# One-hot gate matrices stored token by token, 128 contiguous values a token, with indices and gates in pairs

## The chip, the cores and the metric

The kernel runs on one core of one Trainium2 chip. The metric is the device time of one launch in microseconds (us); lower is better. A core has five engines with instruction streams of their own: TensorE (PE in the views; PEld is its loading of stationary operands, "weights"), VectorE (DVE), ScalarE (ACT), GpSimd (POOL) and SyncE (SP), which here issues the transfers of the weight stream.

## The reference, cut to what matters

A first block (gated mixers and a feed-forward net) is followed by two layers, a retention layer and a latent attention layer, each with a product-key expert net behind it. The change lies in the expert net, which runs twice on 256 tokens. Each token has 8 heads with 16 chosen experts each, so 128 chosen experts of 16384; an expert's number is 128 * i1 + i2.

```
s1, i1 = lax.top_k(s[:, :, 0], PEER_TOPK)
s2, i2 = lax.top_k(s[:, :, 1], PEER_TOPK)
...
top_s, pos = lax.top_k(cand_s, PEER_TOPK)
eidx = jnp.take_along_axis(cand_i, pos, axis=-1)
gate = jax.nn.softmax(top_s, axis=-1).astype(xb.dtype)
h = jax.nn.gelu(jnp.einsum('thkd,td->thk', u[eidx], xb), approximate=False)
return jnp.einsum('thk,thkd->td', gate * h, v[eidx])
```

The kernel does not gather. It computes gelu(u x) for all 16384 experts, multiplies it by a dense gate that is zero for the experts that were not chosen, and multiplies by v.

## The kernel before

The whole net is one program, in an order written out by hand: each engine executes its instructions in the order in which the code emits them. Weights come as units of 128x1024 float32. For each unit SP issues a transfer to `raw` (L138, four units ahead), ScalarE rounds it to `whi` (L149), VectorE subtracts to get the rest `wlo` (L164), and TensorE does three products a tile to get float32 accuracy (L221, L222 and L223 for 256 moving columns, L285 to L287 for 512). Rounding and subtraction run up to two units ahead of the products; `whi` and `wlo` have three buffers each.

`peer` is the expert net of one layer. It has three parts: the query product with the choice of experts in the background (`topk`), a loop over 128 tiles `e` of the u product (24 products each, one unit of weight), and the v product, again 128 units.

`topk` leaves four tiles with a row for each of a token's 128 chosen experts and a column for each of the 256 tokens: `i1h` and `i2h` (the two halves of the expert's number), `gh` and `gl` (the gate as a float16 and the float16 rest). ScalarE writes `i1h`, `i2h` (L1215) and `gh` (L1232) from PSUM, VectorE writes `gl` (L1233).

The dense gate is made beside the u product, four tokens at a time, 64 groups a layer. A group has three steps:

- `g_onehot`, on VectorE, four instructions of 128x512 float16: `o1` is 1 where the first half of the index equals the column's number (L1252), `o2` the same for the second half (L1253), and `ohh` and `ohl` are `o2` times the two parts of the gate (L1254, L1255). `o1`, `ohh` and `ohl` have two buffers, `o2` one. All four have the shape [128, 128, 4]: the value for number i and token j of the four lies at position 4 i + j, so the 128 values of one token are 4 elements (8 bytes) apart.
- `g_mm`, on TensorE, eight products of 128x128 float16: for each of the four tokens `ohh` (L1265) and `ohl` (L1266) are loaded as the stationary operand and `o1` streams as the moving one, both read with that step of 4 elements. The eight go behind the 24 products of one tile `e`.
- `g_evac`, which brings the group's gates out of PSUM: VectorE multiplies them into the tiles of `X` that already hold gelu (L1276), ScalarE copies them to the places of the tiles still to come (L1278).

In tile `e` the code emits the 24 products of `e`, the eight products of the group whose one-hots were built beside the tile before, and then `finish(e - 1)`: gelu on ScalarE (L1294, L1296), the evacuation of the group multiplied beside tile `e - 1`, the one-hots of the next group, and the product of gelu and gate (L1302). Last come the rounding and the subtraction of the weight of tile `e + 2`. One-hots begin once the background work of `topk` is done (about tile 46), and a schedule spreads the 64 groups over the tiles up to 123, so some tiles have none.

A short loop `keep_warm` (L293) elsewhere in the program multiplies a constant float16 tile `idle`, 384 moving columns, with contiguous operands; nobody reads its result.

Of the kernel before, what the change touches and what calls it, by code (L numbers as in the profile page):

```python
# [10 lines left out]
F32 = mybir.dt.float32  # L11
# [19 lines left out]
# weight streams in the order in which they are used: (input, units, columns)  # L31
# [12 lines left out]
# per-feature vectors, one column for each 128 features  # L44
# [13 lines left out]
# constants that depend on the shapes alone  # L58
# [15 lines left out]
# units whose product is one float32 matmul a tile, where VectorE is the busier engine  # L74
# [18 lines left out]
def fused_kernel(ctx: ExitStack, tc: tile.TileContext, a: dict, out: bass.AP):  # L93
# [12 lines left out]
    # ---------------------------------------------------------------- constants  # L106
    cst = const.tile([P, NCST], F32, name="cst")
    vec = const.tile([P, NVEC], F32, name="vec")
    io = const.tile([P, 768], F16, name="io")
    iota4 = io[:, 0:512].rearrange("p (i t) -> p i t", t=4)  # L110
    iota16 = io[:, 512:768].rearrange("p (r k) -> p r k", r=16)
# [15 lines left out]
    # ---------------------------------------------------------------- weight stream  # L127
# [41 lines left out]
    def pump(budget):  # L169
        """emit background work worth the budget in us of VectorE; the work yields its cost, or None when it must wait."""  # L170
        if not bg:
            return
        st["credit"] = min(st["credit"] + budget, 2.0)
        i = 0
        while st["credit"] > 0 and i < len(bg):
            try:
                c = next(bg[i])
            except StopIteration:
                bg.pop(i)
                continue  # L180
            if c is None:
                i += 1
            else:
                st["credit"] -= c

    def drain_bg(*gens):
        """emit all that is left of these generators, or of all of them."""
# [10 lines left out]
    def take(name, i):  # L198
        """the next unit; nothing is split ahead for it."""
# [15 lines left out]
    # ---------------------------------------------------------------- products  # L215
# [3 lines left out]
    def mm3(ps, w, x, start, stop):  # L219
        """ps += w_tile^T x to float32 accuracy, w and x as (hi, lo)."""  # L220
# [4 lines left out]
    def steps(stages, n):  # L225
        """the stages of n items, the later stages of an item emitted beside the earlier ones of the next."""
# [6 lines left out]
    def lin_fm(name, xhl, nk, nf, evac, k0=0, budget=0.0, head=0, produce=None, post=None, i0=0, f_base=0, x32=None):  # L233
        """out^T[f] = sum_k W[k, f]^T x^T[k]; the weight comes as 8 tiles a unit, f major.
        The first `head` output tiles go k by k, as the k tiles of x are produced."""
# [46 lines left out]
    def tm_half(w, ps, o, xh, xl, ncol, first, last):  # L282
        """ps[128 tokens, cols o..o+512] += x[k]^T W[k] for one block of tokens."""
# [5 lines left out]
    def keep_warm(n):  # L289
        """products of a constant that nobody reads: the tensor engine's clock stays up while a norm is worked out."""  # L290
# [4 lines left out]
    def lin_tm(name, x_of, nk, ncol=1024, i0=0, budget=0.0, mid=None, after=None, psb=None, each=None, lead=0, warm=0):  # L295
        """token-major out = x W; x_of(k, b) gives the (hi, lo) stationaries of k tile k, token block b.
        Returns the banks [block][half of the columns]; `mid` comes before the last but one unit, `after` at the end."""
# [23 lines left out]
    # ---------------------------------------------------------------- small pieces  # L321
# [7 lines left out]
    def rstd_of(x, n):  # L329
        """1/sqrt(x) for a small [P, n] tile of positive numbers."""  # L330
# [12 lines left out]
    def table_ready(func=AF.Sqrt):  # L343
        """have the function's table in place."""
        nc.scalar.activation(out=small("rt", 1), in_=eps_t[:, 0:1], func=func)

    def rstd_root(v, scale, eps, ahead=False):
        """1/sqrt(scale * v + eps) for v [P, 2]; ScalarE may round a weight ahead behind the root."""
# [8 lines left out]
    def recip_root(s, x, n):  # L357
        """1/sqrt(x) from s = sqrt(x): the reciprocal and one Newton step."""
# [7 lines left out]
    def ln_coeffs(rows, eps, root=False, ahead=False):  # L366
        """rstd and -mean*rstd [P, 2] of the token-major rows of the two blocks, each in chunks of at most 512."""
# [12 lines left out]
    def coeffs_of(mv, eps, root=False, ahead=False):  # L380
        """the same from mv [P, block, (mean, variance)]."""
# [9 lines left out]
    def rms_coeff(rows, n, eps, junk):  # L391
        """rstd [P, 2] of the mean squares of the token-major rows of the two blocks."""
# [10 lines left out]
    def transposes(src, k, ps):  # L403
        """ps[128 features, 256 tokens] from the token-major src [P, 2, *], feature tile k."""
# [6 lines left out]
    def diags(r, pool):  # L411
        """diagonal matrices of the two columns of r."""
# [7 lines left out]
    def spread(dgs, dst):  # L420
        """dst[:, token] = the diagonals' values, on every partition."""
# [5 lines left out]
    def add_alpha_h(psb, h):  # L427
        """out[token, feature] += ALPHA * h."""
# [13 lines left out]
    class LnTail:  # L442
        """layer norm of token-major PSUM rows into the feature-major h and its split, block by block."""
# [23 lines left out]
    # ================================================================ sin and cos  # L467
    def sincos(ang, sn, cs, pool, n, c1=0.9, c2=1.2):
        """sn, cs of ang >= 0, step by step; ang is overwritten."""
# [18 lines left out]
    # ================================================================ first block  # L488
# [27 lines left out]
    def sq_mm(sq, k, ssp):  # L516
        """ssp[token, block] += sum over the features of tile k."""
# [4 lines left out]
    def rms_of(ssp, n, eps, root=False):  # L522
        """rstd [token, block] from the sums of squares."""
# [31 lines left out]
    # conv branch: a * sigmoid(gate), then the depthwise taps and the statistics in the background  # L555
# [34 lines left out]
    # the same token-major, in the place of the inputs  # L590
# [31 lines left out]
    # pooling branch: token-major here, so that the windows are products over the tokens  # L622
# [28 lines left out]
    def sgu():  # L651
        """mixed^T[c, i] = sum_j v[j, c] w_s[i, j] + b_s, times u; the norm's gain and bias of c are applied to the product."""
# [69 lines left out]
    # pooling branch  # L722
# [23 lines left out]
    # conv branch: layer norm over the channels, silu  # L746
# [16 lines left out]
    class RmsTail:  # L763
        """h_out = h_in + rms_norm(rows) * g, feature-major, from token-major PSUM rows."""
# [23 lines left out]
    # feed-forward; its norm's rstd is applied to the products  # L788
# [56 lines left out]
    # tables of the retention layer, in the background  # L845
    def tables():
# [11 lines left out]
        # log gamma = log1p(-exp(l)), then the decay between key m (partition) and query n  # L858
# [43 lines left out]
    # gated per-layer embedding  # L902
# [42 lines left out]
    # ================================================================ retention  # L945
# [32 lines left out]
    def ret_y(hd, pss):  # L978
        """rows of head hd, token-major"""
# [5 lines left out]
    def ret_n(hd, step):  # L985
        """their norm, in three steps"""
# [11 lines left out]
    def ret_t(f):  # L998
        """feature-major, gated and split: three steps, for feature tiles f, f-1 and f-2"""
# [16 lines left out]
    for hf in range(2):  # L1016
# [8 lines left out]
        if hf == 0:  # L1025
            # scores^T[m, n] * decay
# [26 lines left out]
    # ================================================================ product-key experts  # L1053
    NCAND = 80  # sums of the rank pairs (0, 0..15), (1..7, 0..7), (8..15, 0): they hold the 16 greatest of the 256
    NEG = -3.0e38

    def peer(layer, hl, lt, hm, scope, after_of, mid_of=None, beside_v=()):
        """experts of one layer; lt produces hl during the first product. after_of(X) gives the tail's callback."""
# [6 lines left out]
        def open_x():  # L1065
            # the scope of the mixer ends once its last tile is read
# [49 lines left out]
        def topk():  # L1116
            pp, sc, cv = box["pp"], box["sc"], box["cv"]
            i1h = box["i1h"] = pp.tile([P, T], F16, name="i1h")
            i2h = box["i2h"] = pp.tile([P, T], F16, name="i2h")
            gh = box["gh"] = pp.tile([P, T], F16, name="gh")  # L1120
            gl = box["gl"] = pp.tile([P, T], F16, name="gl")
# [21 lines left out]
            # the first level is done, so its scores' place is free  # L1143
            big = [sc.rearrange("p b g k -> p (b g k)")[:, 1024 * i:1024 * (i + 1)].bitcast(F16).rearrange("p (h r k) -> p h r k", h=8, r=16) for i in range(4)]
            B16 = [P, 8, 16, 16]
            for b in range(2):
# [28 lines left out]
                # the softmax over the 16 begins  # L1175
# [551 lines left out]
```

## Time and profile before

| what | value |
|---|---|
| median of 3 runs | 2569.59 us (2567.75 to 2570.72) |
| span of the profiled execution | 2569.1 us |
| PE busy | 2525.4 us, 98% |
| PEld busy | 2279.2 us, 89% |
| DVE busy | 1818.6 us, 71% |
| ACT busy | 1275.8 us, 50% |
| the tile with a layer's first group of one-hot products begins at | 947.7 and about 1909 us |
| the tile with its last group ends at | 1221 and about 2183 us |

The span runs from the first to the last instruction of the profiled execution; the run times beside it are of other executions of the same program. Busy time of TensorE says little by itself, because products are pipelined and overlap: each record is longer than the distance to the next product's start. The distances between starts are what counts, and they are read from the timeline. Wherever VectorE's instructions follow each other without a wait their records overlap too, by some 0.08 us.

### The profile page before, as it was taken

Reading aid. Unit: us, or ns where it says so; the run is one execution under the profiler, and the core shown is the slowest. Engines: PE = TensorE matmul, PEld = TensorE weight load, DVE = VectorE, ACT = ScalarE, POOL = GpSimd, SP = SyncE. Lnnn points to the kernel's source line nnn. Section 1 sums busy time; section 2 is a strip of 40 time slices with the busy share of each in tenths; the row PEclk is TensorE's granted clock in tenths of the full one; section 3 lists DMA queues with packets and bytes.
Section 4 is the critical chain, followed back from the end, with each engine's and each line's share of the span. In section 5 each row is a group of like instructions: output and inputs, shape, how many; then the busy total and the mean of one; then the engine's idle time right before and its main releaser. Section 6 shows DMA issues by size and latency. Waiting matters only on the chain. (4 is left out here: it accounts for less than half of the span.)

```text
span 2569.1 us, 43426 instructions
## 1 busy us (share of the span) xinstructions
PE 2525.4 (98%) x16903; PEld 2279.2 (89%) x16903; DVE 1818.6 (71%) x3714; ACT 1275.8 (50%) x2161; POOL 9.2 (0%) x21
## 2 busy tenths in 40 slices
PE   8999999999999999999999999999999999999998
PEld 8899899898889999999878887779999999888886
DVE  7988677585757978888555555657977888555555
ACT  4544555553644554444454444544554444444443
POOL 0000000000000000000000000000000000000000
PEclk9999999999999999999999999999999999999999
DMA  6645555555455554444555554534554444655553
GB/s 203 219 141 171 173 174 194 189 195 166 147 165 170 188 187 147 148 148 156 197 186 188 187 188 146 165 116 154 188 189 141 148 149 155 219 188 188 188 186 121
DMA packets 120927, 441.24 MB, mean 172 GB/s; under 512 B 13936, under 2 KB 14320, under 8 KB 119312
## 3 DMA queue, kind: packets, MB, share of 16 engines
q1 hardware_dynamic: 118832, 426.01, 50.6%
q0 software_dynamic: 1888, 12.45, 1.3%
q8 instruction: 132, 2.16, 0.3%
q14 instruction: 75, 0.61, 0.1%
HBM read 433.16 MB, written 5.24 MB: 171 GB/s over the span
## 5 line engine op out<-in xcount | busy, mean ns | idle before, releaser
L164 DVE TENSOR_TENSOR wlo<-raw,whi 128x1024 fp32r<-128x1024 f32 (+1 forms) x797 | 969.1, 1218 | 528.2 <-ACT whi L149 525.7
L149 ACT ACTIVATE whi<-raw 128x1024 fp32r<-128x1024 f32 (+1 forms) x797 | 838.8, 1053 | 722.4 <-PE bank L287 475.4
L221 PE MATMUL bank<-hl,whi 128*128 128x256 f32 x2080 | 594.3, 286 | 4.0 <-ACT hl L550 3.0
L222 PE MATMUL bank<-hl,whi 128*128 128x256 f32 x2080 | 580.4, 279 | 0.3
L223 PE MATMUL bank<-hl,wlo 128*128 128x256 f32 x2080 | 579.9, 279 | 0.3 <-DVE wlo L164 0.3
L285 PE MATMUL bank<-whi,ch 128*128 128x512 f32 x1024 | 405.0, 395 | 1.9 <-ACT ch L323 1.9
L287 PE MATMUL bank<-whi,cl 128*128 128x512 f32 x1024 | 404.8, 395 | 0.1
L286 PE MATMUL bank<-wlo,ch 128*128 128x512 f32 x1024 | 404.5, 395 | 0.0
L221 PEld LDWEIGHTS bank<-hl,whi 128*128 128x128 f32 x2080 | 394.8, 190 | 5.0 <-ACT hl L550 3.3
L222 PEld LDWEIGHTS bank<-hl,whi 128*128 128x128 f32 x2080 | 393.8, 189 | 1.4 <-DVE hl L465 0.5
L223 PEld LDWEIGHTS bank<-hl,wlo 128*128 128x128 f32 x2080 | 392.7, 189 | 1.1 <-DVE wlo L164 0.9
L221 PE MATMUL lps<-hl,whi 128*128 128x256 f32 x1208 | 343.2, 284 | 0.7 <-ACT fhl L834 0.6
L223 PE MATMUL lps<-hl,wlo 128*128 128x256 f32 x1208 | 337.2, 279 | 0.5 <-DVE wlo L164 0.5
L222 PE MATMUL lps<-hl,whi 128*128 128x256 f32 x1208 | 337.0, 279 | 0.0
L285 PEld LDWEIGHTS bank<-whi,ch 128*128 128x128 f32 x1024 | 191.9, 187 | 49.1 <-ACT ch L323 2.7
L287 PEld LDWEIGHTS bank<-whi,cl 128*128 128x128 f32 x1024 | 191.9, 187 | 48.4 <-DVE cl L324 1.8
L286 PEld LDWEIGHTS bank<-wlo,ch 128*128 128x128 f32 x1024 | 191.9, 187 | 47.0
L221 PEld LDWEIGHTS lps<-hl,whi 128*128 128x128 f32 x1208 | 229.0, 190 | 1.5 <-ACT fhl L834 0.7
L223 PEld LDWEIGHTS lps<-hl,wlo 128*128 128x128 f32 x1208 | 229.2, 190 | 0.8 <-DVE wlo L164 0.7
L222 PEld LDWEIGHTS lps<-hl,whi 128*128 128x128 f32 x1208 | 229.2, 190 | 0.3
L1296 ACT ACTIVATE X<-bank 128x256 f32<-128x256 f32 (+33 forms) x246 | 76.4, 310 | 105.5 <-PE bank L223 105.5
L1266 PE MATMUL ax<-o,ohl 128*128 128x128 f16 x512 | 128.6, 297 | 0.0
(420 smaller groups left out, 3113.6 us busy)
## 6 DMA issues: line engine op xcount, KB each, us to landing
raw<-in_p_u_dram SPq DMA_DIRECT2D x256, 512.0 KB, 3.3
raw<-in_p_v_dram SPq DMA_DIRECT2D x256, 512.0 KB, 3.3
raw<-in_w_fi_dram SPq DMA_DIRECT2D x44, 512.0 KB, 3.3
raw<-in_p_q_dram SPq DMA_DIRECT2D x32, 512.0 KB, 3.3
raw<-in_w_gate_dram SPq DMA_DIRECT2D x24, 512.0 KB, 3.3
raw<-in_w_fo_dram SPq DMA_DIRECT2D x22, 512.0 KB, 3.3
raw<-in_w_conv_dram SPq DMA_DIRECT2D x16, 512.0 KB, 4.2
raw<-in_r_qk_dram SPq DMA_DIRECT2D x16, 512.0 KB, 4.1
```

The costliest lines, as they stand in the source:

```text
L149: nc.scalar.activation(out=hi[:, :c], in_=raws[j][:, :c], func=AF.Copy)
L164: nc.vector.tensor_tensor(out=lo[:, :c], in0=r[:, :c], in1=hi[:, :c].bitcast(F32), op=ALU.subtract)
L221: nc.tensor.matmul(ps, w[0], x[0], start=start, stop=False, skip_group_check=True)
L222: nc.tensor.matmul(ps, w[0], x[1], start=False, stop=False, skip_group_check=True)
L223: nc.tensor.matmul(ps, w[1], x[0], start=False, stop=stop, skip_group_check=True)
L285: nc.tensor.matmul(ps[:, :n], xh, w[0][:, o:o + n], start=first, stop=False, skip_group_check=True)
L286: nc.tensor.matmul(ps[:, :n], xh, w[1][:, o:o + n], start=False, stop=False, skip_group_check=True)
L287: nc.tensor.matmul(ps[:, :n], xl, w[0][:, o:o + n], start=False, stop=last, skip_group_check=True)
L1266: nc.tensor.matmul(ps[:, s], ol[:, :, j], o1[:, :, j], start=False, stop=True, skip_group_check=True)
L1296: nc.scalar.activation(out=X[:, e, td:], in_=ps[:, td:T], func=AF.Gelu)
```

## The change

It changes where the values of the one-hots lie, and with them the tiles they are computed from. `o1`, `o2`, `ohh` and `ohl` become [128, 4, 128]: the 128 values of one token are contiguous, and the products of L1273 and L1274 (L1265 and L1266 before) read them so. The table of column numbers is 128 values long instead of each value four times. `i1h`, `i2h`, `gh` and `gl` hold every value twice, side by side, and VectorE reads a pair again and again over the 64 pairs of columns of a token, so the innermost step of all its operands remains one element. The writers of the four tiles write twice as many elements (`twice`); `ei1` and `ei2` use the places of `row` and `col`. The counts and the order of the instructions on every engine are those of before. Comments and docstrings are dropped all over the file; that is left out here.

```
-    io = const.tile([P, 768], F16, name="io")
-    iota4 = io[:, 0:512].rearrange("p (i t) -> p i t", t=4)
+    io = const.tile([P, 384], F16, name="io")
+    iota = io[:, 0:P]
...
-            i1h = box["i1h"] = pp.tile([P, T], F16, name="i1h")
...
+            i1h, i2h, gh, gl = (pp.tile([P, T, 2], F16, name=n) for n in ("i1h", "i2h", "gh", "gl"))
...
+            def twice(x):
+                return x.unsqueeze(2).to_broadcast([P, x.shape[-1], 2])
...
-                ei = [pp.tile([P, 8, 16], F32, tag=t, name=t) for t in ("ei1", "ei2")]
+                ei = [pp.tile([P, 8, 16], F32, tag=t, name=n) for t, n in (("row", "ei1"), ("col", "ei2"))]
...
-                    nc.scalar.activation(out=dst[:, bs], in_=ps[:, i * P:(i + 1) * P], func=AF.Copy)
+                    nc.scalar.activation(out=dst[:, bs, :], in_=twice(ps[:, i * P:(i + 1) * P]), func=AF.Copy)
...
-            nc.scalar.activation(out=gh, in_=ps[:, :T], func=AF.Copy)
-            nc.vector.tensor_tensor(out=gl, in0=ps[:, :T], in1=gh, op=ALU.subtract)
-            yield 0.5
+            nc.scalar.activation(out=gh, in_=twice(ps[:, :T]), func=AF.Copy)
+            nc.vector.tensor_tensor(out=gl, in0=twice(ps[:, :T]), in1=gh, op=ALU.subtract)
+            yield 0.8
...
-            o1, oh_, ol = (pp.tile([P, P, 4], F16, tag=t, name=t, bufs=2) for t in ("o1", "ohh", "ohl"))
-            o2 = pp.tile([P, P, 4], F16, tag="o2", name="o2", bufs=1)
+            o1, oh_, ol = (pp.tile([P, 4, P], F16, tag=t, name=t, bufs=2) for t in ("o1", "ohh", "ohl"))
+            o2 = pp.tile([P, 4, P], F16, tag="o2", name="o2", bufs=1)
...
+            H = [P, 4, P // 2, 2]
+
+            def halves(x):
+                return x.rearrange("p t (i c) -> p t i c", c=2)
 
             def bc(x):
-                return x[:, ts_].unsqueeze(1).to_broadcast([P, P, 4])
-
-            nc.vector.tensor_tensor(out=o1, in0=iota4, in1=bc(box["i1h"]), op=ALU.is_equal)
-            nc.vector.tensor_tensor(out=o2, in0=iota4, in1=bc(box["i2h"]), op=ALU.is_equal)
-            nc.vector.tensor_tensor(out=oh_, in0=o2, in1=bc(box["gh"]), op=ALU.mult)
-            nc.vector.tensor_tensor(out=ol, in0=o2, in1=bc(box["gl"]), op=ALU.mult)
+                return x[:, ts_, :].unsqueeze(2).to_broadcast(H)
+
+            every = iota.rearrange("p (i c) -> p i c", c=2).unsqueeze(1).to_broadcast(H)
+            nc.vector.tensor_tensor(out=halves(o1), in0=every, in1=bc(box["i1h"]), op=ALU.is_equal)
+            nc.vector.tensor_tensor(out=halves(o2), in0=every, in1=bc(box["i2h"]), op=ALU.is_equal)
+            nc.vector.tensor_tensor(out=halves(oh_), in0=halves(o2), in1=bc(box["gh"]), op=ALU.mult)
+            nc.vector.tensor_tensor(out=halves(ol), in0=halves(o2), in1=bc(box["gl"]), op=ALU.mult)
...
-                nc.tensor.matmul(ps[:, s], oh_[:, :, j], o1[:, :, j], start=True, stop=False, skip_group_check=True)
-                nc.tensor.matmul(ps[:, s], ol[:, :, j], o1[:, :, j], start=False, stop=True, skip_group_check=True)
+                nc.tensor.matmul(ps[:, s], oh_[:, j, :], o1[:, j, :], start=True, stop=False, skip_group_check=True)
+                nc.tensor.matmul(ps[:, s], ol[:, j, :], o1[:, j, :], start=False, stop=True, skip_group_check=True)
```

## Rows read from the trace of the kernel before

**Rows 1.** The page: busy time by engine, and granted clock in tenths by slice.

```profile
PE 2525.4 (98%) x16903; PEld 2279.2 (89%) x16903; DVE 1818.6 (71%) x3714; ACT 1275.8 (50%) x2161; POOL 9.2 (0%) x21
...
PEclk9999999999999999999999999999999999999999
```

**Rows 2.** Busy time by stretch: us, PE, PEld, DVE, ACT, POOL, clock, DMA share, GB/s.

```profile
947.70:1221.00 273.30, 273.30 (x2363) 270.12 (x2362) 227.53 (x469) 128.18 (x294) 0.00 (x0) 1.00 0.46 149
1909.00:2183.00 274.00, 274.00 (x2362) 270.86 (x2361) 227.83 (x469) 128.11 (x294) 0.00 (x0) 1.00 0.45 149
```

**Rows 3.** Timeline of PE at tile 47's group: start us, duration us, engine, line.

```profile
950.35 0.28 PE L223 MATMUL bank<-hl,wlo 128*128 128x256 f32 x1
950.47 0.29 PE L1265 MATMUL ax<-o,ohh 128*128 128x128 f16 x1
950.58 0.30 PE L1266 MATMUL ax<-o,ohl 128*128 128x128 f16 x1
950.70 0.30 PE L1265 MATMUL ax<-o,ohh 128*128 128x128 f16 x1
...
951.28 0.29 PE L1266 MATMUL ax<-o,ohl 128*128 128x128 f16 x1
951.33 0.36 PE L221 MATMUL bank<-hl,whi 128*128 128x256 f32 x1
951.53 0.28 PE L222 MATMUL bank<-hl,whi 128*128 128x256 f32 x1
```

**Rows 4.** Timeline of PEld in the same stretch.

```profile
950.47 0.12 PEld L1265 LDWEIGHTS <-ohh 128*128 128x128 f16 x1
950.48 0.13 PEld L1266 LDWEIGHTS <-ohl 128*128 128x128 f16 x1
950.58 0.12 PEld L1265 LDWEIGHTS <-ohh 128*128 128x128 f16 x1
...
951.29 0.21 PEld L221 LDWEIGHTS bank<-hl,whi 128*128 128x128 f32 x1
```

**Rows 5.** Loads and one product by line: count, duration in ns min/median/max, first and last start.

```profile
L1265 PEld LDWEIGHTS <-ohh x512: 113/116/119, 950.5 to 2183.1; 128*128 128x128 f16 x171
...
L293 PEld LDWEIGHTS <-idle x113: 95/98/151, 1.3 to 1714.7; 128*128 128x128 f16 x113
L293 PE MATMUL ax<-idle x113: 326/326/527, 1.3 to 1714.9; 128*128 128x384 f16 x113
...
L519 PEld LDWEIGHTS bank<-cst,sq x32: 187/192/192, 323.5 to 332.4; 128*128 128x128 f32 x32
```

**Rows 6.** Timelines of two other places, rows of one kind merged.

```profile
1711.14 0.99 PE L293 MATMUL ax<-idle 128*128 128x384 f16 x5
...
323.52 0.53 PEld L519 LDWEIGHTS bank<-cst,sq 128*128 128x128 f32 x4
```

**Rows 7.** Timeline of DVE beside tiles 102 to 104.

```profile
1145.50 0.58 DVE L1276 SCALAR_TENSOR_TENSOR X<-ax,X 128x404 f32<-128x404 f32 x1
1145.99 0.42 DVE L1252 TENSOR_TENSOR o<-io,i1h 128x512 f16<-128x512 f16 x1
...
1147.45 0.35 DVE L1302 TENSOR_TENSOR X<-X,gel 128x192 f32<-128x192 f32 x1
1147.72 1.22 DVE L164 TENSOR_TENSOR wlo<-raw,whi 128x1024 fp32r<-128x1024 f32 x1
1149.27 0.58 DVE L1276 SCALAR_TENSOR_TENSOR X<-ax,X 128x408 f32<-128x408 f32 x1 [0.33 <-PE ax L1266]
...
1154.83 1.23 DVE L164 TENSOR_TENSOR wlo<-raw,whi 128x1024 fp32r<-128x1024 f32 x1 [0.58 <-ACT whi L149]
```

**Rows 8.** Groups of VectorE by form: count, busy us, mean ns, idle before.

```profile
L1254 DVE TENSOR_TENSOR ohh<-o,gh 128x512 f16<-128x512 f16 x128 | 54.4, 425 | 4.4
...
L1197 DVE TENSOR_TENSOR X<-r,io 128x2048 f16<-128x2048 f16 x8 | 9.7, 1217 | 0.0
...
L700 DVE TENSOR_TENSOR merged<-merged,brt 128x256 f32<-128x256 f32 x16 | 6.8, 425 | 0.5
```

**Rows 9.** The writer of `gl` by line, columns as in Rows 5.

```profile
L1233 DVE TENSOR_TENSOR gl<-ax,gh x2: 425/425/425, 940.5 to 1902.1; 128x256 f16<-128x256 f32 x2
```

**Rows 10.** Two stretches of the u product without one-hot products, columns as in Rows 2.

```profile
830.00:886.00 56.00, 56.00 (x478) 56.00 (x477) 54.78 (x209) 30.11 (x42) 0.00 (x0) 1.00 0.59 190
893.00:925.00 32.00, 32.00 (x283) 31.89 (x282) 30.06 (x99) 19.17 (x27) 0.00 (x0) 1.00 0.57 186
```

More of the change, by code (lines that the diff above doesn't have):

```diff
@@ L108, in fused_kernel @@
     vec = const.tile([P, NVEC], F32, name="vec")
-    io = const.tile([P, 768], F16, name="io")
-    iota4 = io[:, 0:512].rearrange("p (i t) -> p i t", t=4)
-    iota16 = io[:, 512:768].rearrange("p (r k) -> p r k", r=16)
+    io = const.tile([P, 384], F16, name="io")
+    iota = io[:, 0:P]
+    iota16 = io[:, P:384].rearrange("p (r k) -> p r k", r=16)
     idle = const.tile([P, 384], F16, name="idle")
@@ L1117, in topk @@
             pp, sc, cv = box["pp"], box["sc"], box["cv"]
-            i1h = box["i1h"] = pp.tile([P, T], F16, name="i1h")
-            i2h = box["i2h"] = pp.tile([P, T], F16, name="i2h")
-            gh = box["gh"] = pp.tile([P, T], F16, name="gh")
-            gl = box["gl"] = pp.tile([P, T], F16, name="gl")
+            i1h, i2h, gh, gl = (pp.tile([P, T, 2], F16, name=n) for n in ("i1h", "i2h", "gh", "gl"))
+            box.update(i1h=i1h, i2h=i2h, gh=gh, gl=gl)
+            def twice(x):
+                return x.unsqueeze(2).to_broadcast([P, x.shape[-1], 2])
             for g in range(16):
@@ L1706, in _layout @@
     a.update(_constants())
-    a["io"] = np.tile(np.concatenate([np.repeat(np.arange(P, dtype=np.float16), 4), np.repeat(np.arange(16, dtype=np.float16), 16)]), (P, 1))
+    a["io"] = np.tile(np.concatenate([np.arange(P, dtype=np.float16), np.repeat(np.arange(16, dtype=np.float16), 16)]), (P, 1))
     return {k: np.ascontiguousarray(x) for k, x in a.items()}
```

## The prediction

> **What bounds the kernel now.** I read the page first. TensorE is busy for 98% of the span at the full granted clock in every slice [rows 1], so it sets the time and no clock change is to be had. Then I asked where the one-hot products run: in two stretches of 273.3 and 274.0 us, in which PE has no idle time at all and VectorE is busy for 227.5 and 227.8 us, 83%, ScalarE for 128 us [rows 2]. So a gain on PE there is kept only as far as VectorE, the second busiest engine, can follow.
>
> In the timeline of PE the distance between starts is the cost. The eight products of a group start 0.117 us apart (950.47 to 951.28 is 0.81 for seven distances) [rows 3], though each has only 128 moving columns. The float32 products beside them have 256 columns and start 0.113 us apart (32.00 us for 283) or 0.117 us apart (56.00 us for 478) [rows 10]. And the constant products of `keep_warm`, also float16 with a load each, but contiguous, take five times 384 columns in 0.99 us, the last record being 0.33 us long [rows 5, 6]: (0.99 - 0.33) / 4 = 0.165 us for 384 columns, 0.055 us for 128. A one-hot column therefore costs twice what a contiguous float16 column costs.
>
> **The change part by part.** It moves no instruction; it changes what four products a token read and how wide a few writers are.
>
> The spacing of the products. What holds them to 0.117 us? Either the reading of the moving operand, or the load of the stationary one. The loads: a one-hot load's record is 116 ns, the contiguous one's 98 ns [rows 5]. But a record is longer than the time for which a load blocks the next one: four float32 loads of 192 ns each follow each other within 0.53 us, so (0.53 - 0.19) / 3 = 0.113 us apart [rows 5, 6], 0.08 us less than the record. Taking 0.08 off, a one-hot load blocks for some 0.036 us and a contiguous one for 0.018 us, neither near 0.117. The second load of a group starts 0.01 us after the first [rows 4], which says the same. So the load is slower with the step of 4 elements, by a factor of two, but it is hidden; what is left is the moving operand, read with the same step. I take the contiguous price, 0.055 us, since the `keep_warm` rows are the nearest: same type, same load width, contiguous. The bounds of this term are 0.055 us and today's 0.117 us; nothing makes contiguous reading slower than strided, so no loss here.
>
> The sum for a group. Today, from the start of the L223 product ahead of it (950.35) to the start of L222 behind it (951.53), it is 1.18 us [rows 3]; two distances of float32 products, some 0.115 us each [rows 10], belong to those products themselves. The group costs 0.95 us. After the change: 0.01 us for the first load; seven distances of 0.055 us, 0.385 us; and behind the eighth product L221 has to wait for its own float32 load, which begins when the eighth product starts (951.29) [rows 4] and blocks for 0.113 us. That is 0.51 us, 0.44 us less. Two layers of 64 groups: 128 times 0.44 is 56.3 us, all of it on PE, which has no idle time in these stretches.
>
> What is late next: VectorE. A tile's work on it at tile 102 runs from 1145.50 to the end of the subtraction at 1148.94, 3.44 us, or 3.36 us when the next instruction follows without a wait and overlaps by 0.08 us; today it then waits 0.33 us for the group's last product [rows 7]. PE's tile with a group shrinks from some 3.69 us (24 times 0.115 plus 0.95 is 3.71) to 3.27 us, below VectorE's 3.36 us. Tiles without one-hots give time back: beside tile 104 VectorE needs 3.1 us (1152.97 to 1156.06) with 0.58 us of that a wait for ScalarE [rows 7]. In total 227.5 us of work and about 13 such waits of 0.6 us, 235 us, have to fit into 273.3 - 28.2 = 245 us [rows 2]. They fit, but from about tile 100 on VectorE falls behind by 0.1 us a tile. Subtractions run up to two tiles ahead, so some 3 us of lag do not reach PE. I put the cost at 0 to 6 us over both layers and take 3.
>
> The one-hots themselves. Four instructions of 128x512 float16 at 425 ns stay four of the same size [rows 8]. The operand that was read in runs of four elements is read in runs of two. The trace has no run of two; the nearest rows are these with runs of four, and a 2048-element one with runs of sixteen, 1217 ns [rows 8]. Both fit one line: 792 ns more for 1536 elements more, so no cost of short runs shows down to four. I take 0. The other end is a fall to the float32 rate; it is the rival below. A gain isn't excluded by the rows, but with equal counts I know no source of one.
>
> The writers. `gl` grows from 256 to 512 elements a layer; VectorE's float32 slope, (1220 - 425) / 768 = 1.03 ns an element between 256 and 1024 [rows 7, 8], makes it 425 + 265 = 690 ns [rows 9]. It runs at 940.5, the first group's product at 950.47 [rows 3, 9]; 10 us cover it and the few tenths of the ScalarE copies. Without that cover all of them would cost about 1 us a layer. The index table's smaller transfer and the shared places of `ei1` and `ei2` lie off the path: 0.
>
> One more spread: float32 products pace at 0.113 or 0.117 us [rows 10] without any change in their instructions, and which of the two holds can turn at each group. 77 tiles of 24 products in two layers, 3696 products, times 0.004 us is 15 us from all slow to all fast. Today's stretch lies in between, since (273.3 - 64 x 0.95) / 1848 = 0.115 us [rows 2]; so 7 us either way, with no reason for a direction.
>
> Sum: 2569.1 - 56.3 + 3 = 2515.8 us for the span. The median of the runs is 0.5 us above the profiled span, so 2516 us.
>
> **The rivals.**
>
> *Load and product do not overlap.* Then a pair costs the 0.055 us of its columns and the 0.018 us for which a contiguous load blocks, 0.073 us. For it: the contiguous loads of the trace all hide behind products of 384 columns, 0.165 us [rows 6], and none of 128 contiguous columns is there. Against it: the strided pair's 0.117 us has room to hide a load of 0.036 us. A group then costs 0.01 + 0.51 + 0.113 = 0.63 us, 0.32 us less than today, 41 us in all: 2529 us. [...]
>
> *The load's whole record sets the distance.* For it: record and distance are equal today, 116 and 117 ns, and the next product starts just when the record ends [rows 3 to 5]. Against it: the float32 loads above, which follow each other well inside their records. Then 98 ns replace 116 ns, 0.15 us a group, 19 us: 2550 us.
>
> *No change.* The step isn't the cause, and 0.117 us is what any pair costs on this path. For it: no pair in these rows goes below 0.11 us, float32 ones included. Against it: those have 256 columns or a float32 load to account for it; and the strided load is longer than the contiguous one, so the step does cost something. 2569 us. [...]
>
> *Slower: the one-hots lose half their rate.* The four instructions now write in steps of a pair with operands of four dimensions. If VectorE handles this at the rate of float32, 512 elements take 690 ns by the slope above in place of 425, 1.06 us a group. VectorE's 235 us become 303 us a layer, and it sets the end: 30 us more than 273.3, 60 us in both layers, 2629 us. It bites from about 40 ns an instruction (10 us of room in 256 instructions) and turns the gain into a loss from about 150 ns (38 us of room today). For it: 256 float32 elements take the same 425 ns as 512 float16 [rows 8], so there is such a rate to fall to, and no row shows runs of two. Against it: the innermost step is one element everywhere, and today's runs of four are read at the full rate although they repeat as well.
>
> **How the numbers follow.** Forecast 0.59, overlap missing 0.13, load's record 0.10, no change 0.08, half rate 0.10. The forecast's own range is 2501 to 2530: 56.3 us of gain, 3 us either way for VectorE, 7 us for the float32 pace, and a little for the group's ends. To hold 8 in 10 the range reaches over the next two cases: 2500 to 2553 us. Faster by over 0.2% (5 us, about what a measurement of this kernel can tell from no change): 0.59 + 0.13 + 0.10 = 0.82. Within it 0.08, slower 0.10.
>
> **What would show it.** In the profile after: distances of 0.055 us between the group's products (0.073, 0.098 or 0.117 by the rivals); a load record near 98 ns; one-hot instructions at 415 to 425 ns (690 by the last rival); stretches of 245 to 250 us; less idle time of VectorE ahead of the evacuations, and PE waiting on `wlo` in the last 25 tiles of the u product if VectorE's lag exceeds its reserve. The forecast is wrong if the distance stays above 0.08 us or if a one-hot instruction takes over 0.47 us.

## The result

| kernel | median, us | range (runs) | profiled execution, span |
|---|---|---|---|
| before, same chip | 2570.15 | 2567.75 to 2571.37 (4) | 2569.1 (the one of the rows above) |
| after | 2527.36 | 2525.46 to 2531.11 (4) | 2524.3 |

The ratio of the times is 0.9837, 95% interval 0.9825 to 0.9849: the change makes the kernel 1.6% faster. The forecast was 2516 us, in a range of 2500 to 2553. So the sign and the mechanism held, and 11 us of the expected 54 are missing. The rest of this document asks what carried the gain and where the 11 us went. Of these, 8.5 us are in the span of the profiled execution (2524.3 us, forecast 2515.8); the other 2.6 us are the distance from that span to the median of the runs, which the prediction put at 0.5 us and which is 3.1 us here.

### The profile page after: what moved, and what is told of

Read it like the earlier page. It is cut to its first block, busy times and chain, and to the rows that moved or that the text cites. A ratio compares the mean times of both kernels' runs of the same rounds, so it can differ in the third digit from the quotient of the medians.

```text
span 2524.3 us, 43428 instructions
## 1 busy us (share of the span) xinstructions
PE 2482.1 (98%) x16903; PEld 2236.3 (89%) x16903; DVE 1815.6 (72%) x3714; ACT 1276.8 (51%) x2161; POOL 9.2 (0%) x21
## 4 chain that ended last, share of the span: by engine, by line
PE 82%; issue 13%; DMA 2%; ACT 2%; DVE 1%; SPq 0%; POOL 0%; POOLq 0%; ACTq 0%; DVEq 0%
PE bank L287 11%; PE bank L285 11%; PE bank L286 11%; PE bank L221 10%; PE bank L222 10%; PE bank L223 10%; PE lps L221 4%; PE lps L222 4%; PE lps L223 4%; PE lps L270 2%; PE ax L1273 1%; PE ax L1274 1%; DMA X<-in_keys_dram 1%; PE ax L1112 1%; ACT whi L149 1%
## 5 line engine op out<-in xcount | busy, mean ns | idle before, releaser
L222 PE MATMUL bank<-hl,whi 128*128 128x256 f32 x2080 | 584.7, 281 | 0.3
L223 PE MATMUL bank<-hl,wlo 128*128 128x256 f32 x2080 | 584.4, 281 | 0.3 <-DVE wlo L164 0.3
L222 PEld LDWEIGHTS bank<-hl,whi 128*128 128x128 f32 x2080 | 395.4, 190 | 1.4 <-DVE hl L465 0.5
L223 PEld LDWEIGHTS bank<-hl,wlo 128*128 128x128 f32 x2080 | 392.7, 189 | 1.0 <-DVE wlo L164 0.9
L223 PE MATMUL lps<-hl,wlo 128*128 128x256 f32 x1208 | 337.1, 279 | 0.5 <-DVE wlo L164 0.5
L222 PE MATMUL lps<-hl,whi 128*128 128x256 f32 x1208 | 336.9, 279 | 0.0
L222 PEld LDWEIGHTS lps<-hl,whi 128*128 128x128 f32 x1208 | 229.5, 190 | 0.3
L223 PEld LDWEIGHTS lps<-hl,wlo 128*128 128x128 f32 x1208 | 228.7, 189 | 0.8 <-DVE wlo L164 0.7
L1302 ACT ACTIVATE gel<-bank 128x84 f32<-128x84 f32 (+47 forms) x154 | 44.0, 286 | 178.6 <-PE bank L223 178.6
```

Of the source, the lines that this page charges most:

```text
L222: nc.tensor.matmul(ps, w[0], x[1], start=False, stop=False, skip_group_check=True)
L223: nc.tensor.matmul(ps, w[1], x[0], start=False, stop=stop, skip_group_check=True)
L1302: nc.scalar.activation(out=gl_[:, 0:td], in_=ps[:, 0:td], func=AF.Gelu)
```

## The profile after

The page's busy times (us, share of the span, instructions), and the two stretches from a layer's first product of tile 47 to that of tile 124, columns as in [rows 2]:

```profile
PE 2482.1 (98%) x16903; PEld 2236.3 (89%) x16903; DVE 1815.6 (72%) x3714; ACT 1276.8 (51%) x2161; POOL 9.2 (0%) x21
```
```profile
951.86:1202.39 250.53, 250.53 (x2362) 247.71 (x2361) 226.07 (x469) 127.94 (x294) 0.00 (x0) 1.00 0.50 163
1887.64:2138.17 250.53, 250.53 (x2362) 247.70 (x2361) 226.01 (x469) 127.93 (x294) 0.00 (x0) 1.00 0.50 163
```

PE still has no idle time there, with the same products; the same 77 tiles took 273.25 and 274.02 us before (the stretches of [rows 2], within 0.05 us). The stretches shrank by 46.2 us, the span by 44.8. The other 1.4 us were lost elsewhere: tiles 0 to 46, which have no group, took 1.55 us more (133.12 before and 134.45 after in the first layer, 133.13 and 133.35 in the second), the rest of the program 0.15 us less. On TensorE nothing is changed in those tiles.

The timeline of PE at the group behind tile 47 answers to [rows 3], and shows the start and the end of the float32 products of tile 48 too:

```profile
954.47 0.28 PE L223 MATMUL bank<-hl,wlo 128*128 128x256 f32 x1
954.59 0.23 PE L1273 MATMUL ax<-o,ohh 128*128 128x128 f16 x1
954.65 0.22 PE L1274 MATMUL ax<-o,ohl 128*128 128x128 f16 x1
954.71 0.22 PE L1273 MATMUL ax<-o,ohh 128*128 128x128 f16 x1
...
954.99 0.22 PE L1274 MATMUL ax<-o,ohl 128*128 128x128 f16 x1
955.02 0.36 PE L221 MATMUL bank<-hl,whi 128*128 128x256 f32 x1
955.22 0.28 PE L222 MATMUL bank<-hl,whi 128*128 128x256 f32 x1
...
955.57 0.28 PE L222 MATMUL bank<-hl,whi 128*128 128x256 f32 x1
...
957.69 0.28 PE L222 MATMUL bank<-hl,whi 128*128 128x256 f32 x1
```

Seven distances take 0.40 us: 0.057 us each where [rows 3] had 0.117. From the start of L223 ahead of the group to L222 behind it, it is 0.75 us instead of 1.18. The two last rows are six rounds of three products apart: 2.12 / 18 = 0.118 us a product.

Loads and products of the line by form (answers to [rows 5]), and the one-hot instructions and the writer of `gl` on VectorE by form (answer to [rows 8, 9]: count, busy us, mean ns, idle before):

```profile
L1273 PEld LDWEIGHTS <-ohh x512: 96/98/98, 954.6 to 2138.0; 128*128 128x128 f16 x171
L1273 PE MATMUL ax<-o,ohh x512: 219/219/230, 954.6 to 2138.1; 128*128 128x128 f16 x171
```
```profile
L1262 DVE TENSOR_TENSOR ohh<-o,gh 128x512 f16<-128x512 f16 x128 | 54.4, 425 | 4.4
L1261 DVE TENSOR_TENSOR o<-io,i2h 128x512 f16<-128x512 f16 x128 | 53.5, 418 | 0.0
...
L1236 DVE TENSOR_TENSOR gl<-ax,gh 128x512 f16<-128x512 f32 x2 | 1.4, 691 | 2.6 <-ACT gh L1235 2.6
```

A load's record is 98 ns, an instruction with pairs costs what one with runs of four did, and `gl` costs the 0.69 us that the float32 slope gave. VectorE's waits for a group's products (us in total, times, longest), first before and then after:

```profile
DVE X L1276 <- PE ax L1266: 62.6, 117, 1.1
```
```profile
DVE X L1284 <- PE ax L1274: 16.0, 58, 0.6
```

VectorE lost 47 us of waiting, about the gain of the two stretches: TensorE came nearer to it, and the trace shows no wait of PE for `wlo` in these tiles.

## The experiments

Each kernel is the changed one with one edit. A run is the float32 products between one group and the next. "At 113" counts the runs that go at 113 to 114 ns a product; the rest go at 118. "Stretch" is the time of tiles 47 to 123, first and second layer. Ratios are against the kernel before on the same chip.

| kernel | median, us (range) | ratio [95%] | stretch, us | at 113 |
|---|---|---|---|---|
| before | 2570.15 (2567.75 to 2571.37) | 1 | 273.25, 274.02 | 83 of 128 |
| after | 2527.36 (2525.46 to 2531.11) | 0.9837 [0.9825, 0.9849] | 250.53, 250.53 | 0 of 128 |
| `after_again` | 2525.24 (2523.46 to 2527.08) | 0.9816 [0.9793, 0.9838] | 250.53, 250.64 | 0 of 128 |
| `moving_stepped` | 2576.62 (2557.74 to 2584.52) | 1.0015 [0.9991, 1.0040] | 269.9, 277.3 | 64 of 128 |
| `loads_stepped` | 2519.48 (2518.00 to 2524.48) | 0.9801 [0.9777, 0.9825] | 248.68, 248.59 | 63 of 128 |
| `no_pairs` | 2626.35 (2624.74 to 2627.28) | 1.0209 [1.0187, 1.0232] | 300.75, 300.52 | runs broken by waits |
| `half_products` | 2501.51 (2495.65 to 2506.01) | 0.9723 [0.9702, 0.9743] | 237.27, 237.24 | 1 of 120 unbroken |
| `fill256` | 2517.65 (2512.59 to 2520.39) | 0.9786 [0.9769, 0.9803] | 247.73, 247.73 | 128 of 128 |
| `fill32` | 2521.13 (2519.37 to 2523.45) | 0.9803 [0.9787, 0.9819] | 247.31, 247.31 | 128 of 128 |
| `seven_products` | 2509.72 (2508.16 to 2516.88) | 0.9772 [0.9748, 0.9796] | 243.79, 243.79 | 64 of 128 |
| `fill32_twice` | 2523.30 (2518.65 to 2524.67) | 0.9812 [0.9792, 0.9832] | 249.02, 249.02 | 128 of 128 |
| `fill32_first` | 2520.55 (2517.55 to 2522.86) | 0.9805 [0.9785, 0.9825] | 248.91, 249.02 | 64 of 128 |
| `fill_once` | 2524.73 (2521.02 to 2529.48) | 0.9830 [0.9804, 0.9856] | 250.50, 250.50 | 2 of 128 |
| `ninth_onehot` | 2519.64 (2518.19 to 2524.87) | 0.9810 [0.9784, 0.9837] | 247.73, 247.73 | 128 of 128 |

### The changed kernel once more

> The changed kernel once more, beside the others on one chip. All theories expect what was measured, 2525 to 2531 us, distances of 0.056 us between the eight products of a group. On the pace of the 24 float32 products behind a group two theories differ: if a group with contiguous operands always leaves them in the slower of their two paces (0.117 us), all 128 groups show it again; if the pace is chance, some of the 128 show 0.113 us.

Again all 128 runs go at 118 ns, and the stretches repeat to 0.1 us. Tiles 0 to 46 do not repeat so well: in the first and second layer they take 134.45 and 133.35 us in the profiled execution of after, 132.21 and 134.43 us here. The 1.4 us lost outside the stretches are within that spread.

### Which operand's step held the products at 0.117 us

In one kernel only the moving operand `o1` keeps the step of four elements; the constant tile of `keep_warm` is halved there to make room. In the other only the two stationary operands keep it.

```
-                nc.tensor.matmul(ps[:, s], oh_[:, j, :], o1[:, j, :], start=True, stop=False, skip_group_check=True)
+                nc.tensor.matmul(ps[:, s], oh_[:, j, :], o1[:, :, j], start=True, stop=False, skip_group_check=True)
```

> The changed kernel, but the moving operand o1 lies as before, stepped by four elements; ohh and ohl, the loaded operands, are contiguous. If reading the moving operand sets the distance, the eight products stay 0.117 us apart although the load record falls to 98 ns, and the time is near the kernel before, 2560 to 2572 us. If the load sets it, the distance is 0.056 us and the time 2525 to 2531 us.

```
-                nc.tensor.matmul(ps[:, s], oh_[:, j, :], o1[:, j, :], start=True, stop=False, skip_group_check=True)
+                nc.tensor.matmul(ps[:, s], oh_[:, :, j], o1[:, j, :], start=True, stop=False, skip_group_check=True)
```

> The changed kernel, but the loaded operands ohh and ohl lie as before, stepped by four elements, and only the moving operand o1 is contiguous. If reading the moving operand sets the distance, the products are 0.056 us apart with load records of 116 ns, and the time is that of the changed kernel, 2525 to 2531 us. If the load sets it, the distance is 0.117 us and the time 2560 to 2572 us. If load and product share the time, it lies between: 0.036 + 0.056 = 0.092 us, 2549 us.

Timeline of PE and its loads by line with `o1` stepped, then the same for the loads stepped:

```profile
950.06 0.29 PE L1279 MATMUL ax<-o,ohh 128*128 128x128 f16 x1
950.17 0.30 PE L1280 MATMUL ax<-o,ohl 128*128 128x128 f16 x1
950.29 0.30 PE L1279 MATMUL ax<-o,ohh 128*128 128x128 f16 x1
```
```profile
L1279 PEld LDWEIGHTS <-ohh x512: 96/116/118, 949.8 to 2181.6; 128*128 128x128 f16 x171
```
```profile
951.49 0.25 PE L1282 MATMUL ax<-o,ohh 128*128 128x128 f16 x1
951.57 0.22 PE L1283 MATMUL ax<-o,ohl 128*128 128x128 f16 x1
951.63 0.22 PE L1282 MATMUL ax<-o,ohh 128*128 128x128 f16 x1
...
954.99 0.22 PE L1282 MATMUL ax<-o,ohh 128*128 128x128 f16 x1
955.05 0.22 PE L1283 MATMUL ax<-o,ohl 128*128 128x128 f16 x1
955.10 0.22 PE L1282 MATMUL ax<-o,ohh 128*128 128x128 f16 x1
```
```profile
L1282 PEld LDWEIGHTS <-ohh x512: 112/113/116, 951.5 to 2131.2; 128*128 128x128 f16 x171
```

With only `o1` stepped the whole gain is gone (0.116 us a product, ratio 1.0015; the two stretches take 547.2 us, 547.3 before). With only the loads stepped it is there: 0.056 us between products, save the first two of a group, which start 0.083 us apart on average (0.067 in the changed kernel), 2.2 us in all 128 groups. So the gain comes from the moving operand's step, but for those 2.2 us. The median of `moving_stepped`, 2576.62 us, lies above the expected 2560 to 2572, and its runs spread over 27 us; the two paces of the float32 products alone put 7 us between its two layers. The load records add a correction. Contiguous loads beside a stepped product read 116 ns; the shortest, 96 ns, are first loads of groups, which have no stepped product beside them. The record thus also holds time that depends on the product beside it, and the step itself costs a load 15 ns (113 against 98), hidden for all loads of a group but the first, by the distances above.

`loads_stepped` is also some 6 us below `after_again` on the same chip (ranges that overlap by 1 us), with stretches 1.9 us shorter. Its one-hot products go at the same distance; what differs is that 63 of its 128 runs go at 113 ns.

### What the pairs are for

Here indices and gates stand once, and VectorE reads each of them 128 times with a step of zero:

```
-                return x[:, ts_, :].unsqueeze(2).to_broadcast(H)
+                return x[:, ts_].unsqueeze(2).to_broadcast([P, 4, P])
```

> The changed kernel without the pairs: indices and gates are stored once a token and read with step zero along the 128 values of a token. If VectorE then works at the float32 rate, each of the four one-hot instructions takes about 690 ns in place of 420, VectorE has 231 + 64 x 1.06 = 299 us of work and some 8 us of waits in a stretch that lasts 250.5 us now, becomes the bound, and the time rises by 2 x 56 us to some 2640 us. If step zero is as fast as pairs, the time stays at 2525 to 2531 us and the pairs were not needed.

The one-hot instructions by form, and the largest wait of PE:

```profile
L1262 DVE TENSOR_TENSOR ohh<-o,gh 128x512 f16<-128x512 f16 x128 | 88.6, 692 | 4.4
L1263 DVE TENSOR_TENSOR ohl<-o,gl 128x512 f16<-128x512 f16 x128 | 87.6, 684 | 0.0
```
```profile
PE bank L223 <- DVE wlo L164: 51.8, 115, 0.6
```

An instruction costs 681 to 692 ns instead of 415 to 425, VectorE sets the end, and PE waits for `wlo`. That is the rival of the half rate, at the price that the prediction gave it (690 ns and 2629 us; 2626.35 measured); the 2640 us expected of this run were 14 us too many. The new layout without the pairs would have lost 2%, and the kernel after shows that a run of two is enough: the instruction that writes `ohh` takes 692 ns with an innermost step of zero and 425 with a step of one.

### How far VectorE can follow

The `ol` products are left out, so the gates lack their low part:

```
-                nc.tensor.matmul(ps[:, s], ol[:, j, :], o1[:, j, :], start=False, stop=True, skip_group_check=True)
```

> The changed kernel without its second product of each token: four products a group in place of eight, so the gates lack their low part (ol is still built). TensorE-bound theory: 128 groups x 4 products x 0.056 us = 28.7 us less than the changed kernel's 2525 to 2527, so 2497 to 2498 us, if the float32 products keep the slower pace of 117 to 118 ns, down to some 2482 if they turn to 113 ns. Rival, VectorE nearly binds: its 231 us of work and some 8 us of waits for ScalarE leave no more than 12 to 18 us a layer below the changed kernel's 257 us; then it holds the stretch at 239 us or more and the time stays at 2500 us or above, with TensorE waiting for wlo.

Four products less take 0.22 us from a tile: up to tile 113 a tile between two groups takes 3.120 us where the changed kernel has 3.343. Then VectorE holds it: some of the tiles from 114 on take up to 3.51 us in the first layer and 3.38 in the second. In the first of them L223, the product that reads `wlo`, starts 0.40 us behind L222 instead of 0.12, and 0.06 us after the end of a subtraction on VectorE:

```profile
1159.17 1.22 DVE L164 TENSOR_TENSOR wlo<-raw,whi 128x1024 fp32r<-128x1024 f32 x1
```
```profile
1160.05 0.28 PE L222 MATMUL bank<-hl,whi 128*128 128x256 f32 x1
1160.45 0.39 PE L223 MATMUL bank<-hl,wlo 128*128 128x256 f32 x1
```

The gain of a stretch is 13.3 us instead of 64 x 0.224 = 14.3. So VectorE was near, but it costs only 1 us a layer even at 3.12 us a tile. TensorE binds up to the last tiles, as the first expectation has it. The stretches, 237.3 us, are shorter than the rival's 239; the time, 2501.5 us (2495.7 to 2506.0), is above its 2500 but cannot tell the two apart.

### Which pace the float32 products take

The pace of 118 ns behind every group was the one thing in the profile after that no step had foreseen. Seven kernels ask what sets it. The first idea was the cover of the first float32 load: a long product ahead of it, tried with 256 and, as a control, 32 columns of the constant tile, written to the part of the tile's bank that nobody reads.

```
                 g_mm()
                 more = 1
+                nc.tensor.matmul(ps[:, T:T + 256], idle[:, 0:P], idle[:, 0:256], start=True, stop=True, skip_group_check=True)
```

> The changed kernel with one more product behind each group: 128x128 by 256 contiguous columns of the constant float16 tile, into the part of the tile's bank that nobody reads. It tests why all 128 runs of float32 products behind a group go at 117 to 118 ns in the changed kernel. Theory: the first float32 load behind the group has nothing long enough beside it, so the float32 products start load-bound and stay so; a product of 256 columns covers that load, as other products with long streams do which are followed by 113 ns. Then the 128 runs go at 113 ns: the filler costs some 0.057 us a group net of what it covers (7 us), the pace gives up to 15 us back, about 2518 us. Rival, the pace has another cause: all 128 runs stay at 117 to 118 ns, and the time is 2530 to 2539 us.

> The control of the kernel with the filler of 256 columns: the same product with 32 columns, too short to cover a float32 load of 113 ns. Theory of the cover: the runs of float32 products stay at 117 to 118 ns and the time is 2529 to 2533 us (0.03 to 0.06 us a group more). If the runs turn to 113 ns here too, it is not the cover that decides, but any change of the distance at which the float32 products begin; then 2513 to 2520 us.

Both turn all 128 runs to 113 ns. The theory of the cover expected 2518 us from the first, and 2517.65 were measured, but the reason is wrong: 32 columns do the same. Next came the count of products and their place: one product less (the low part of each fourth token is left out), two of the short ones, and one ahead of the group.

```
-                nc.tensor.matmul(ps[:, s], ol[:, j, :], o1[:, j, :], start=False, stop=True, skip_group_check=True)
+                if j < 3:
+                    nc.tensor.matmul(ps[:, s], ol[:, j, :], o1[:, j, :], start=False, stop=True, skip_group_check=True)
```

> The changed kernel without the low product of each group's fourth token: seven products a group in place of eight, nothing added. It asks what turned the float32 products to 113 ns behind all 128 groups when a ninth product was added behind each group (32 or 256 columns alike), while eight and four products leave them at 117 to 118 ns. Theory of the odd count: seven products turn them to 113 ns as well; 128 x 0.056 = 7 us for the products and 128 x 0.09 = 11 us for the pace come off the changed kernel's 2525 to 2527 us, about 2508 us. Rival, what stands directly ahead of the float32 products decides (the constant tile, another bank, the shorter stream): they stay at 117 to 118 ns and only the 7 us come off, about 2519 us.

> The changed kernel with two products of 32 constant columns behind each group, ten in all. Theory of the odd count: an even number, so the 128 runs behind groups go at 117 to 118 ns again: 128 x (0.10 to 0.12) us is added and nothing given back, 2538 to 2542 us. Rival, what stands directly ahead decides: the runs go at 113 ns as with one such product, 0.05 us a group more than with one, 2525 to 2529 us.

> The changed kernel with one product of 32 constant columns ahead of each group instead of behind it: nine products in all, and what stands directly ahead of the float32 products is a one-hot product as in the changed kernel. Theory of the odd count: the 128 runs go at 113 ns, 2518 to 2522 us, as with the product behind the group. Rival, what stands directly ahead decides: 117 to 118 ns, 0.05 us a group more, 2531 to 2534 us.

With seven products, and with nine of which the constant one goes first, the runs alternate strictly, 118, 113, 118 and so on. Neither theory had that; that the two times, 2509.72 and 2520.55 us, lie near what the odd count expected (2508, and 2518 to 2522) is luck. Timeline of PE with seven products, first and last L222 of the same 18 distances in two tiles that follow each other:

```profile
953.83 0.28 PE L222 MATMUL bank<-hl,whi 128*128 128x256 f32 x1
...
955.95 0.28 PE L222 MATMUL bank<-hl,whi 128*128 128x256 f32 x1
...
957.13 0.28 PE L222 MATMUL bank<-hl,whi 128*128 128x256 f32 x1
...
959.17 0.28 PE L222 MATMUL bank<-hl,whi 128*128 128x256 f32 x1
```

2.12 us, and then 2.04: 0.118 and 0.113 us a product. With ten products, the last two constant, all runs go at 113 ns: an even count doesn't bring the 118 back. The last two kernels ask whether a pace once reached is kept (one constant product, behind the first group only), and whether the kind of the ninth product matters or its place (it repeats the eighth, into the tile's own bank).

```
+                if gst["mm"] == 1:
+                    nc.tensor.matmul(ps[:, T:T + 32], idle[:, 0:P], idle[:, 0:32], start=True, stop=True, skip_group_check=True)
```

> The changed kernel with one product of 32 constant columns behind the first group of each layer only. It asks whether the pace of the float32 products, once at 113 ns, is kept by the groups of eight that follow. Theory that an even count keeps the pace (four, eight and ten products gave one pace for all groups, seven, and nine with the constant product ahead, alternated): all 128 runs at 113 ns, 0.087 us less for each of 64 tiles with and 13 without a group in a layer, some 13 us: 2512 to 2514 us. Rival, eight contiguous products lead to 117 to 118 ns whatever was before them (in the changed kernel the products ahead of the first group go at 113 ns in both layers, and those behind it at 118): only the first group's run is quick, 2525 to 2527 us.

```
+                nc.tensor.matmul(ps[:, T:T + P], g9[1], g9[0], start=True, stop=True, skip_group_check=True)
```

> The changed kernel with a ninth product behind each group that repeats the eighth (128 one-hot columns with ohl of the fourth token), but into the unused part of the tile's own bank, where the constant product stood that turned all 128 runs to 113 ns. If the count decides, the runs alternate as with seven products and with nine whose constant product stands ahead, 64 at 113 ns and 64 at 117 to 118: 7 us for the products, some 7 us given back, 2524 to 2528 us. If the place decides (the bank that is written last, before the float32 products), all 128 go at 113 ns: 2518 to 2521 us.

The pace isn't kept. Timeline of PE in `fill_once`, the tile behind the constant product and the next, the same 18 distances:

```profile
950.30 0.18 PE L1326 MATMUL bank<-idle 128*128 128x32 f16 x1
...
950.88 0.28 PE L222 MATMUL bank<-hl,whi 128*128 128x256 f32 x1
...
952.92 0.28 PE L222 MATMUL bank<-hl,whi 128*128 128x256 f32 x1
...
954.14 0.28 PE L222 MATMUL bank<-hl,whi 128*128 128x256 f32 x1
...
956.26 0.28 PE L222 MATMUL bank<-hl,whi 128*128 128x256 f32 x1
```

2.04 us behind the constant product, 2.12 behind the next group of eight, and so in both layers. The tile at 113 ns takes 3.257 us, the next 3.344: the pace is worth 0.087 us a tile. And the repeated one-hot product acts like the constant one. Timeline of PE in `ninth_onehot`:

```profile
953.54 0.22 PE L1326 MATMUL bank<-o,ohl 128*128 128x128 f16 x1
...
954.13 0.28 PE L222 MATMUL bank<-hl,whi 128*128 128x256 f32 x1
...
956.17 0.28 PE L222 MATMUL bank<-hl,whi 128*128 128x256 f32 x1
```

What is shown: where the last product ahead of the float32 ones wrote to the spare part of the finished tile's bank, all 514 runs of five kernels go at 113 to 114 ns, whatever its columns (32, 128, 256) and its operands. Where the last product wrote to the `ax` bank, eight contiguous products lead to 118 ns, from either pace, four do so in 119 of the 120 runs without a wait, and seven or nine alternate. The granted clock does not tell the paces apart: in the first layer's stretch it is 1.00 in after, where all runs go at 118 ns, and 1.00 in `fill256`, where all go at 113. What stays open: why. The destination was never changed alone, with eight products, and with stepped operands the pace follows yet other sequences (83 and 63 of 128 in before and `loads_stepped`); in `moving_stepped` all 64 groups of a layer keep the pace that stood ahead of the first, 113 ns and 118 ns.

As versions of the kernel, `fill256` and `loads_stepped` have the lowest medians of those that compute all of the gates: the stretches are 2.8 and 1.9 us a layer shorter than after, and the ratios 0.9786 and 0.9801. `fill32` and `ninth_onehot` lie so near (3.2 and 2.8 us a layer, ratios 0.9803 and 0.9810) that none is shown to be the best. The interval of `fill256` lies below that of after (0.9837) and overlaps that of `after_again` (0.9816) a little; by the stretches it gains some 6 us, with a product added that does nothing.

## Why the prediction was right, and where it was off

**The spacing.** Forecast 0.055 us, measured 0.056 to 0.057. The nearest row, contiguous products of 384 columns, gave the right price per column, and the two kernels with one stepped operand each show that the moving operand was the cause. The inference on the loads (slower by the step, but hidden) held, but for the first load of a group. The step's price, 18 ns by the rows of 116 and 98, came from loads beside different products; measured with the moving operand contiguous it is 15 ns. The factor of two rests on the 0.08 us that were taken off both, which no run tests.

**The group.** Forecast 0.51 us; measured 0.75 less two distances of 0.118, 0.514. Summed over the starts in the two stretches, from L223 ahead of a group to L222 behind it, the gain is 55.8 us of the forecast 56.3.

**The pace of the float32 products: the term that was mis-sized.** The prediction saw both paces and took 0, with 7 us either way, "with no reason for a direction". The edit did give it a direction. Behind the groups 83 of 128 runs went at 113 ns before, and none after. The other distances between float32 products in the two stretches, 3442 of them, grew from 395.5 to 405.0 us in sum, 0.1149 to 0.1177 us each: 9.6 us were given back, and 55.8 - 9.6 is the 46.2 us measured. The 7 us were too narrow as well, since the slower pace was taken as 0.117 us and is 0.1178.

**VectorE.** Forecast a loss of 3 us (0 to 6); none is seen. At 3.34 us a tile instead of the expected 3.27 TensorE left it more time, but the 3 us would have been too much at 3.27 as well: at 3.12 us, in `half_products`, VectorE cost 2 us in both layers together. What the estimate missed, the reserve of two tiles or the time that tiles without a group give back, no run takes apart.

**One-hots, writers.** 415 to 425 ns and 0.69 us for `gl`, as forecast; no cost of the writers shows in the span.

**The rivals.** The load's whole record (98 ns a product) and no overlap (73 ns) fall with 56 ns. "No change" falls with `moving_stepped`: a step of four 2-byte elements doubles the cost of the moving operand, 116 ns against 56. Half rate is not a price of pairs (415 to 425 ns an instruction), but of reading one value with a step of zero (681 to 692 ns in `no_pairs`).

In sum: -55.8 (forecast -56.3) + 9.6 (forecast 0) + 0 (forecast 3) + 1.4 us elsewhere (forecast 0) is -44.8 us, the change of the span; forecast were -53.3. That VectorE cost nothing hid 3 us of the pace's 9.6.

## What to carry to other kernels

Read the distance between starts of products and hold it against contiguous ones of the same type, per column: where the moving operand is stepped, as here (116 against 56 ns), laying it out contiguously can be worth its cost elsewhere, and the stationary operand can stay stepped as long as its load hides (the step cost 2.2 us in 128 groups here). Keep the innermost step at one on VectorE when a value is repeated; storing it twice was enough here (415 to 425 ns, against 681 to 692 with a step of zero). And where thousands of identical products set the time, put a price on their pace changing by 4% in either direction, because an edit beside them can move it as one (3442 distances from 0.1149 to 0.1177 us here, 9.6 us).

## What the runs showed of the hardware

- Products with float32 operands and 256 columns went at one of two paces here, 0.113 to 0.114 or 0.118 us, through the whole run up to the next group. Which one it is shows within the first seven products of a run that no wait breaks; a product of 32, 128 or 256 columns that writes to the finished tile's own bank just ahead gives 0.113 to 0.114 in all 514 runs here.
- A float16 moving operand with a step of four elements cost twice its contiguous price (116 against 56 ns for 128 columns); a stationary one with the same step 15 ns of load (113 against 98), hidden but for the first load of a group (its first two products started 0.083 us apart, 0.067 in after).
- A load's record is not set by the load alone: 96 to 98 ns beside contiguous products, 116 ns beside stepped ones, for the same contiguous tile (`ohh` in after and in `moving_stepped`).
